# One loaded array for the input and the first block's weights, and the norm's squares two pulls later

## The chip, the cores and the metric

The kernel runs on one core of one Trainium2 chip. The metric is the device time of one execution in microseconds. Five engines work side by side, each through its own instructions in order: TensorE (PE, with its weight loads shown as PEld), VectorE (DVE), ScalarE (ACT), GpSimd (POOL) and SyncE (SP), which here issues nearly all transfers from memory.

## What is computed

One layer of a decoder trunk on 256 tokens of width 2048. All branches read the same normalised input; their gated results are summed, projected and added to the input, and a last norm closes it. Cut to what matters:

```
h = rmsnorm(x, norm_gain)
z = h @ w_in                          # split into q, k, v, gates ... of three branches
o_a = gated linear attention          # (gq, gk, gv, decay)
o_b = forgetting attention            # (fq, fk, fv, forget gate)
o_c = attention into 256 memory tokens: rmsnorm(mem) @ w_mem_kv
y = sum of sigmoid(merge) * (o_branch * silu(gate)) @ w_branch
return rmsnorm(x + y @ w_out, final_gain)
```

All data are fp32. The kernel multiplies in a reduced fp32 form and keeps the precision by splitting each operand in two: `hi` is the rounded value, `lo = raw - hi` the rest, and a product is the sum of three matmuls (hi by hi, hi by lo, lo by hi).

## The kernel before

All large products are 34 **blocks**: 512 columns of a weight matrix, 2048 rows deep, that is 16 **slices** of 128 rows (`KT`). They run in the order of the list `ORDER` (line 45); block 0 is `gq`, block 1 `gk`, blocks 2 and 3 `gv`. `wall` holds the weights as (block, 128, 16, 512). The stream works on quarters of a block (4 slices, 1 MB): `w_load` (line 144) allots a tile `raw`, of which there are 3, and SyncE loads it; `w_cast` (155) has ScalarE write `hi` of half a quarter (2 slices), `w_sub` (179) has VectorE write `lo`. There are 4 `hi` and 4 `lo` buffers. When `lo` of a quarter's second half is issued, the load three quarters ahead follows. In one engine's queue the order is that of issue in the code; SyncE sends no later load while an earlier one waits for its buffer.

`natural` (211) and `transposed` (226) are the matmul loops. `transposed` with `group=1` (block 0) does, slice by slice, four matmuls with `hi` (line 254) and four with `lo` (259), one of each per quarter of the output columns. With `group=4` (block 1) it takes four slices as a group and goes through the four output quarters; each quarter is a step of 4 matmuls with `hi` and 4 with `lo`, two of the latter from each pair of slices.

What is not a large product is written as generators in three lanes (`post`, `side`, `main`). After each slice or step the loop calls `pull()`, which takes each lane's next piece up to its `yield`; `yield 5` lets five pulls pass. So a number after `yield` sets where, between the matmuls, the next instructions are issued.

Block 0 is special: the input has to be split as well. `first_piece` (389) loads, for each pair of slices, the transposed input `xT` into a 4 KB buffer of the pool `apool` (14 of them, `a4`) and the block's weights into `raw` tiles, in two DMAs per slice or pair of slices; the first slice's weights come in two halves. ScalarE then writes the input's high part (`high_x`, line 358), scaled by the gain, and `hi` of the weights (130); VectorE the low parts (361, 131). Block 0's quarters take `raw` tiles too, so the three loads of block 1 that `w_load(6)` issues at the end of block 0's pieces wait for the tiles of quarters 1, 2 and 3.

The norm's factor per token needs the sum of squares of `x` in its natural layout (`xn`). `rms_of` (307) loads the first 128 tokens as two tiles of 128x1024, lets 5 pulls pass, squares both on ScalarE (318), loads the second 128 tokens, lets 5 pulls pass and squares these. The same routine serves the memory tokens (`memn`) about 100 us later. The results are applied behind the products (`scale_T`). Around the first squares, `post` holds the end of block 0: ScalarE copies each quarter of `gq` out (241), VectorE adds the other half (244).

The tiles tagged `m12_0` to `m12_3` (8 KB per partition each) hold the split memory tokens from `load_mem` on (374), and later the branches' outputs.

At the end, `residual` (1044) adds the input and squares with a running sum into `fs`, and `finish` (1058) makes the last norm's factor: VectorE adds the last sum to the earlier ones and scales (1066), ScalarE takes the root (1067), VectorE the reciprocal and one Newton step (1069 to 1071), and the output tiles are scaled and stored.

Of the kernel before, what the change touches and what calls it, by code (L numbers as in the profile page):

```python
# [10 lines left out]
F32 = mybir.dt.float32  # L11
# [48 lines left out]
@with_exitstack  # L60
def body(ctx, tc, xT, memT, xn, memn, wall, wsm, wup, cst, fgain, out):
    nc = tc.nc
# [81 lines left out]
    def w_load(upto):  # L144

        while done[0] <= min(upto, 4 * N_STREAM + 1):
            i, q = divmod(done[0], 4)
            raws[done[0]] = wpool.tile([P, 4, NB], F32, tag="raw", name=nm("raw"), bufs=3)
            if i == N_STREAM:
                q += 2  # L150
            if i:
                nc.sync.dma_start(raws[done[0]], wall[i, :, 4 * q:4 * q + 4, :])
            done[0] += 1

    def w_cast(upto):

        while done[1] <= min(upto, 8 * N_STREAM + 3):
# [8 lines left out]
            if q < 4:  # L166
                lo = wpool.tile([P, 2, NB], F32R, tag="lo", name=nm("lo"))
                first_piece(q, s, raws[q], hi, lo)
                done[2] += 1
                parts[n] = [hi, lo]  # L170
                if n == 7:
                    w_load(6)
            else:
                nc.scalar.copy(hi, raws[q][:, 2 * s:2 * s + 2, :])  # L174
                parts[n] = [hi]
# [131 lines left out]
    def rms_of(src, col, stage):  # L307

        ssq = spool.tile([P, NT, 2], F32, tag="ssq", name=nm("ssq"))
        for t in range(NT):  # L310
            held = []
            for c in range(2):
                raw = stage()
                nc.sync.dma_start(raw, src[:, t, c * 1024:(c + 1) * 1024])
                held.append(raw)
            yield 5
            for c in range(2):
                nc.scalar.activation(held[c], held[c], AF.Square, accum_out=ssq[:, t, c:c + 1])
                yield 1
        ms = spool.tile([P, NT], F32, tag="ms", name=nm("ms"))  # L320
# [20 lines left out]
    nc.gpsimd.memset(warm, 1.0)  # L341
    x12, xraws = [], []

# [44 lines left out]

    def first_piece(g, s, raw, hi, lo):

        if s == 0:
            xraws.append(a4([P, 4, S]))
            x12.append(new_h("x12_", g))
        step = 1 if g < 2 else 2
        for k in range(0, 2, step):
            ks = slice(2 * s + k, 2 * s + k + step)
            kts = slice(4 * g + ks.start, 4 * g + ks.stop)
            nc.sync.dma_start(xraws[g][:, ks, :], xT[:, kts, :])
            cut = (0, 256, NB) if kts.start == 0 else (0, NB)
            for a, b in zip(cut, cut[1:]):  # L400
                nc.sync.dma_start(raw[:, ks, a:b], wall[0, :, kts, a:b])
            for j in range(ks.start, ks.stop):
                kt = 4 * g + j
                high_x(x12[g], xraws[g][:, j, :], j, cs[:, C_GAIN + kt:C_GAIN + kt + 1])
                low_x(x12[g], xraws[g][:, j, :], j, cs[:, C_GAIN + kt:C_GAIN + kt + 1])
                for a, b in zip(cut, cut[1:]):
                    split_w(raw[:, j, a:b], hi[:, j - 2 * s, a:b], lo[:, j - 2 * s, a:b])
        if (g, s) == (2, 1):
            nc.sync.dma_start(wsr, wsm)
            nc.sync.dma_start(w3r, wup)  # L410
# [631 lines left out]
    fs = [cpool.tile([P, 6], F32, name=f"fs{t}") for t in range(NT)]  # L1042

    def residual(n, t, ps, sl, i):

        xt = xr[n][:, t, sl]
        nc.vector.tensor_tensor(out=xt, in0=ps, in1=xt, op=ALU.add)
        sq = a2([P, NB])
        nc.scalar.activation(sq[:, sl], xt, AF.Square, accum_out=fs[t][:, i:i + 1])
        g = fg[n // 2][:, (n % 2) * NB + sl.start:(n % 2) * NB + sl.stop]  # L1050
        nc.vector.tensor_tensor(out=xt, in0=xt, in1=g, op=ALU.mult)

    def residual_in_psum(n, t, ps, sl, i):

        sq = a2([P, NB])
        nc.scalar.activation(sq[:, sl], ps, AF.Square, accum_out=fs[t][:, i:i + 1])

    def finish(t, n_sums, last=None):

        f = spool.tile([P, 6], F32, tag="fin", name=nm("fin"))
        prev, m, neg, r, u, rr = (f[:, i:i + 1] for i in range(6))
        nc.vector.tensor_reduce(prev, fs[t][:, :n_sums - 1], AX.X, ALU.add)
        nc.vector.tensor_scalar(prev, prev, D * EPS, None, ALU.add)
        nc.vector.tensor_scalar(m, fs[t][:, n_sums - 1:n_sums], prev, 4.0 / D, ALU.add, ALU.mult)
        nc.scalar.activation(r, m, AF.Sqrt)
        nc.vector.tensor_scalar(neg, m, -1.0, None, ALU.mult)
        nc.vector.reciprocal(r, r)
# [29 lines left out]
    def late_loads():  # L1099
# [3 lines left out]
        def last_quarter(q):  # L1103

            held.append(hpool.tile([P, 4, NB], F32, tag="mx"[q] + "12_3", name=nm("lraw")))
            nc.sync.dma_start(held[q], wall[len(ORDER) - 1, :, 4 * q:4 * q + 4, :])

# [74 lines left out]
def _layout(inp):  # L1182
# [10 lines left out]
    blocks = [mats[m][:, o:o + NB] for m, o in ORDER]  # L1193
    wall = np.empty((len(blocks), P, KT, NB), np.float32)
    for i, b in enumerate(blocks):
        wall[i] = kp(b)
# [13 lines left out]
    return {  # L1210
        "xT": kp(x.T), "memT": kp(mem.T), "xn": nat(x), "memn": nat(mem), "wall": wall,
        "wsm": wsm, "wup": wup.reshape(96, 512), "cst": cst, "fgain": g["final_gain"][None, :],
# [16 lines left out]
```

## Time and profile before

| | us |
|---|---|
| median of 3 runs | 814.37 |
| lowest and highest | 813.76 and 817.84 |
| profiled execution, its own time | 814.85 |
| its span, first to last instruction | 812.6 |
| TensorE busy in it | 800.5 |
| granted TensorE clock | 0.997 |

A row of the order of time gives the start and the duration in us, the engine, the line of the kernel, the operation, output and inputs, and how many such instructions follow each other; in brackets stands how long the engine had been idle and what ended that. `SPq` is SyncE's queue: the moment at which a load is sent, not its landing. A row of the waits gives who waited for whom, the sum in us, the times and the longest.

### The profile page before, as it was taken

What the parts mean: (1) busy time and instruction counts of PE and PEld (TensorE: products, weight loads), DVE (VectorE), ACT (ScalarE), POOL (GpSimd) and SP (SyncE); (2) the same over time, 40 slices, a digit from 0 to 9 for tenths busy, and PEclk for the clock granted to TensorE, in tenths of its full rate; (3) what the DMA queues carried; (4) which work ended last, traced back from release to release, by engine and by line L of the source; (5) the groups of instructions that cost most, each with busy time, mean ns of one, the idle gap of its engine ahead of it and who ended that gap; (6) DMA issues with size and microseconds to landing.
All of it is one profiled execution on the core that took longest, in us unless ns stands there. A gap on an engine that the chain in (4) does not pass through costs nothing.

```text
span 812.6 us, 9971 instructions
## 1 busy us (share of the span) xinstructions
PE 800.5 (99%) x3888; PEld 673.5 (83%) x3888; DVE 499.0 (61%) x705; ACT 405.2 (50%) x558; POOL 22.6 (3%) x44
## 2 busy tenths in 40 slices
PE   9999999999999999999999999999999999999995
PEld 7788888888888788888888888888888888888885
DVE  6757979885656566667445744465446544575653
ACT  6758646644445465564444444444443444444631
POOL 7000000100000000000000000000000000000000
PEclk9999999999999999999999999999999999999998
DMA  8965647553443444455555455555555555548633
GB/s 279 384 238 181 233 157 253 184 197 144 156 167 145 155 160 151 161 202 193 181 196 207 161 201 208 191 179 199 196 178 196 198 177 195 207 163 308 233 125 104
DMA packets 27439, 157.31 MB, mean 194 GB/s; under 512 B 3216, under 2 KB 4640, under 8 KB 10496
## 3 DMA queue, kind: packets, MB, share of 16 engines
q1 hardware_dynamic: 27120, 156.64, 54.2%
q8 instruction: 30, 0.49, 0.2%
q14 instruction: 17, 0.14, 0.1%
q10 hardware_dynamic: 144, 0.02, 0.0%
q0 software_dynamic: 128, 0.02, 0.0%
HBM read 154.55 MB, written 2.10 MB: 193 GB/s over the span
## 4 chain that ended last, share of the span: by engine, by line
PE 91%; DVE 3%; DMA 3%; ACT 2%; issue 1%; SPq 1%; DVEq 0%; ACTq 0%
PE acc L224 19%; PE acc L226 19%; PE acc L225 19%; PE acc L254 12%; PE acc L259 6%; PE acc L1094 4%; PE acc L1093 4%; PE acc L1095 4%; DMA raw<-wall 2%; PE att L705 1%; DMA a<-xn 1%; DVE lo L187 1%; PE att L441 0%; PE att L1006 0%; PE att L782 0%
## 5 line engine op out<-in xcount | busy, mean ns | idle before, releaser
L187 DVE TENSOR_TENSOR lo<-raw,hi 128x1024 fp32r<-128x1024 f32 x256 | 312.3, 1223 | 200.0 <-ACT hi L174 199.9
L174 ACT CAST hi<-raw 128x1024 fp32r<-128x1024 f32 x256 | 266.4, 1052 | 323.0 <-PE acc L226 238.7
L224 PE MATMUL acc<-hi,x 128*128 128x512 f32 x544 | 214.8, 395 | 0.0
L225 PE MATMUL acc<-lo,x 128*128 128x512 f32 x544 | 212.0, 390 | 0.0
L226 PE MATMUL acc<-hi,x 128*128 128x512 f32 x544 | 211.9, 390 | 0.0
L226 PEld LDWEIGHTS acc<-hi,x 128*128 128x128 f32 x544 | 102.1, 188 | 21.6
L225 PEld LDWEIGHTS acc<-lo,x 128*128 128x128 f32 x544 | 102.2, 188 | 20.8 <-DVE lo L187 0.4
L224 PEld LDWEIGHTS acc<-hi,x 128*128 128x128 f32 x544 | 102.2, 188 | 20.6 <-issue 0.3
L254 PE MATMUL acc<-x,hi 128*128 128x512 f32 x384 | 108.1, 403 | 0.0
L254 PEld LDWEIGHTS acc<-x,hi 128*128 128x128 f32 x384 | 66.8, 189 | 9.9 <-issue 0.3
L259 PEld LDWEIGHTS acc<-x,lo 128*128 128x128 f32 x384 | 58.9, 188 | 10.3 <-DVE lo L187 2.1
L259 PE MATMUL acc<-x,lo 128*128 128x256 f32 x384 | 61.5, 281 | 1.7 <-DVE lo L187 1.7
L224 PE MATMUL acc<-hi,oT 128*128 128x512 f32 x128 | 49.8, 389 | 0.0
L225 PE MATMUL acc<-lo,oT 128*128 128x512 f32 x128 | 49.8, 389 | 0.0
L226 PE MATMUL acc<-hi,oT 128*128 128x512 f32 x128 | 49.8, 389 | 0.0
L1093 PE MATMUL acc<-hi,a 128*128 128x512 f32 x96 | 37.5, 391 | 0.0
L1095 PE MATMUL acc<-hi,a 128*128 128x512 f32 x96 | 37.4, 389 | 0.0
L1094 PE MATMUL acc<-lo,a 128*128 128x512 f32 x96 | 37.4, 389 | 0.0
L225 PEld LDWEIGHTS acc<-lo,oT 128*128 128x128 f32 x128 | 24.0, 188 | 5.0
L226 PEld LDWEIGHTS acc<-hi,oT 128*128 128x128 f32 x128 | 24.0, 188 | 5.0
L224 PEld LDWEIGHTS acc<-hi,oT 128*128 128x128 f32 x128 | 24.0, 188 | 5.0
L1095 PEld LDWEIGHTS acc<-hi,a 128*128 128x128 f32 x96 | 18.0, 188 | 3.8
(221 smaller groups left out, 770.1 us busy)
## 6 DMA issues: line engine op xcount, KB each, us to landing
raw<-wall SPq DMA_DIRECT2D x130, 1024.0 KB, 4.7
a<-xn SPq DMA_DIRECT2D x8, 512.0 KB, 7.5
raw<-wall SPq DMA_DIRECT2D x4, 512.0 KB, 8.0
a<-memT SPq DMA_DIRECT2D x4, 512.0 KB, 6.2
a<-memn SPq DMA_DIRECT2D x4, 512.0 KB, 7.1
lraw<-wall SPq DMA_DIRECT2D x2, 1024.0 KB, 7.5
out<-a SPq DMA_DIRECT2D x8, 256.0 KB, 3.1
raw<-wall SPq DMA_DIRECT2D x7, 256.0 KB, 4.6
```

What stands on the lines that cost most here:

```text
L174: nc.scalar.copy(hi, raws[q][:, 2 * s:2 * s + 2, :])
L187: nc.vector.tensor_tensor(out=lo, in0=raws[q][:, 2 * s:2 * s + 2, :], in1=parts[n][0].bitcast(F32), op=ALU.subtract)
L224: MM(ps[t], lhsT=h1, rhs=hi, start=(kt == first), stop=False)
L225: MM(ps[t], lhsT=h1, rhs=lo, start=False, stop=False)
L226: MM(ps[t], lhsT=h2, rhs=hi, start=False, stop=(kt == last))
L254: MM(ps[c], lhsT=hi[:, c * P:(c + 1) * P], rhs=h_of(h, kt).rearrange("p a s -> p (a s)"), start=(kt == 0), stop=False, skip_group_check=True)
L259: MM(ps[c][:, :S], lhsT=lo[:, c * P:(c + 1) * P], rhs=h_of(h, kt)[:, 0, :], start=False, stop=(kt == KT - 1), skip_group_check=True)
L705: MM(ps[:, j, :], lhsT=E[:, e * P:(e + 1) * P], rhs=Qs[c // 2][:, e % 4, :], start=True, stop=True)
L1093: MM(ps, lhsT=h1, rhs=hi, start=(kt == 0), stop=False)
L1094: MM(ps, lhsT=h1, rhs=lo, start=False, stop=False)
L1095: MM(ps, lhsT=h2, rhs=hi, start=False, stop=(kt == KT - 1))
```

## The change

The input and block 0's weights now lie side by side in one array `xw` of (128, 16, 768): per slice and partition 256 values of the input and 512 of the weights. `wall` loses block 0. `first_piece` loads them together: slice 0 in three DMAs as before (input, two halves of the weights), slices 1 to 7 in one DMA of 384 KB each, slices 8 to 15 in four of 768 KB. They land in the four places `m12_0` to `m12_3`, two slices in each, so each place is filled twice before the memory tokens come. The buffers for `xT` and block 0's use of the `raw` tiles are gone.

`rms_of` issues the second pair of loads before the first squares and holds four tiles at once: loads, 5 pulls, loads, 2 pulls, two squares, 4 pulls, two squares. The first pair of squares is thus issued two pulls later and the second pair at the pull where it stood.

`finish` gets its factor 4/D from the squares (`scale=SQ`). The square root reads the last sum directly and takes the earlier ones, with epsilon, as its bias; one VectorE operation is gone, and VectorE's negated sum stands beside the root.

```
 def w_load(upto):
         while done[0] <= min(upto, 4 * N_STREAM + 1):
             i, q = divmod(done[0], 4)
-            raws[done[0]] = wpool.tile([P, 4, NB], F32, tag="raw", name=nm("raw"), bufs=3)
...
             if i:
-                nc.sync.dma_start(raws[done[0]], wall[i, :, 4 * q:4 * q + 4, :])
+                raws[done[0]] = wpool.tile([P, 4, NB], F32, tag="raw", name=nm("raw"), bufs=3)
+                nc.sync.dma_start(raws[done[0]], wall[i - 1, :, 4 * q:4 * q + 4, :])
...
 def rms_of(src, col, stage):
-        for t in range(NT):
-            held = []
+        held = []
+        for wait in (5, 2):
+            t = len(held) // 2
             for c in range(2):
-                raw = stage()
-                nc.sync.dma_start(raw, src[:, t, c * 1024:(c + 1) * 1024])
-                held.append(raw)
-            yield 5
-            for c in range(2):
-                nc.scalar.activation(held[c], held[c], AF.Square, accum_out=ssq[:, t, c:c + 1])
-                yield 1
+                held.append(stage())
+                nc.sync.dma_start(held[-1], src[:, t, c * 1024:(c + 1) * 1024])
+            yield wait
+        for i, raw in enumerate(held):
+            nc.scalar.activation(raw, raw, AF.Square, accum_out=ssq[:, i // 2, i % 2:i % 2 + 1])
+            yield (1, 4, 1, 1)[i]
...
-    def first_piece(g, s, raw, hi, lo):
+    def first_piece(g, s, hi, lo):
...
-            xraws.append(a4([P, 4, S]))
...
+        p = 2 * g + s
+        both = hpool.tile([P, 8 * S], F32, tag=f"m12_{p % 4}", name=nm("xw"))
+        both = both[:, :6 * S].rearrange("p (k c) -> p k c", k=2)
         step = 1 if g < 2 else 2
         for k in range(0, 2, step):
-            nc.sync.dma_start(xraws[g][:, ks, :], xT[:, kts, :])
-            cut = (0, 256, NB) if kts.start == 0 else (0, NB)
+            cut = (0, S, 2 * S, 3 * S) if kts.start == 0 else (0, 3 * S)
             for a, b in zip(cut, cut[1:]):
-                nc.sync.dma_start(raw[:, ks, a:b], wall[0, :, kts, a:b])
+                nc.sync.dma_start(both[:, ks, a:b], xw[:, kts, a:b])
...
 def finish(t, n_sums, last=None):
-        nc.vector.tensor_scalar(prev, prev, D * EPS, None, ALU.add)
-        nc.vector.tensor_scalar(m, fs[t][:, n_sums - 1:n_sums], prev, 4.0 / D, ALU.add, ALU.mult)
-        nc.scalar.activation(r, m, AF.Sqrt)
-        nc.vector.tensor_scalar(neg, m, -1.0, None, ALU.mult)
+        nc.vector.tensor_scalar(prev, prev, 4.0 * EPS, None, ALU.add)
+        nc.scalar.activation(r, fs[t][:, n_sums - 1:n_sums], AF.Sqrt, bias=prev)
+        nc.vector.tensor_scalar(neg, fs[t][:, n_sums - 1:n_sums], prev, -1.0, ALU.add, ALU.mult)
```

What this moves on ScalarE at the end of block 0: before, from the first copy of `gq` (`a_109`) out of its sums (`att`) on; `hi` is a cast of block 1's weights, `a_348` and `a_350` are the first two tiles of `xn`, and `ssq` their sums of squares.

```order
L241 COPY a_109<-att_175 128x256
L174 CAST hi_425<-raw_309 128x1024
L318 ACTIVATE a_348,ssq_347<-a_348 128x1024
L241 COPY a_109<-att_177 128x256
L318 ACTIVATE a_350,ssq_347<-a_350 128x1024
L241 COPY a_109<-att_179 128x256
L241 COPY a_109<-att_181 128x256
L436 CAST w_100<-b_99 96x512
L174 CAST hi_489<-raw_311 128x1024
```

The same stretch of ScalarE after the change, where `a_337` and `a_339` are the two tiles of `xn`:

```order
L241 COPY a_109<-att_168 128x256
L174 CAST hi_414<-raw_298 128x1024
L241 COPY a_109<-att_170 128x256
L241 COPY a_109<-att_172 128x256
L318 ACTIVATE a_337,ssq_336<-a_337 128x1024
L241 COPY a_109<-att_174 128x256
L438 CAST w_100<-b_99 96x512
L318 ACTIVATE a_339,ssq_336<-a_339 128x1024
L174 CAST hi_478<-raw_300 128x1024
```

The second and third copy now stand ahead of the first square, the fourth and the cast of `w` ahead of the second. VectorE's order is the same in both kernels here.

SyncE's queue before, from the input and weights of slices 12 and 13 on; `raw_307` to `raw_311` are block 1's first three quarters, `raw_376` its last:

```order
L398 DMA a_267<-xT 128x512
L401 DMA raw_264<-wall 128x1024
L398 DMA a_267<-xT 128x512
L401 DMA raw_264<-wall 128x1024
L152 DMA raw_307<-wall 128x2048
L152 DMA raw_309<-wall 128x2048
L152 DMA raw_311<-wall 128x2048
L314 DMA a_348<-xn 128x1024
L314 DMA a_350<-xn 128x1024
L152 DMA raw_376<-wall 128x2048
L314 DMA a_468<-xn 128x1024
```

And after the change, from slices 8 and 9 on; `wsr` and `b` are the small weights:

```order
L402 DMA xw_199<-xw 128x1536
L402 DMA xw_227<-xw 128x1536
L411 DMA wsr<-wsm 128x384
L412 DMA b_99<-wup 96x512
L402 DMA xw_258<-xw 128x1536
L402 DMA xw_286<-xw 128x1536
L152 DMA raw_296<-wall 128x2048
L152 DMA raw_298<-wall 128x2048
L152 DMA raw_300<-wall 128x2048
L315 DMA a_337<-xn 128x1024
L315 DMA a_339<-xn 128x1024
L152 DMA raw_365<-wall 128x2048
```

The order of what follows block 0 is the same; the eight DMAs of its last eight slices are four. In the queue of the memory tokens' norm, the third and fourth `memn` load now stand ahead of a `raw` load that stood ahead of them.

37 lines of the change are left out of this document (19 added, 18 removed).

## The prediction

> **What bounds the kernel now.** I read the page first, then who waited for whom, then the stretches of TensorE, then the order of time around each stretch in which TensorE was not full.
>
> ```profile
> PE 800.5 (99%) x3888; PEld 673.5 (83%) x3888; DVE 499.0 (61%) x705; ACT 405.2 (50%) x558; POOL 22.6 (3%) x44
> ```
> ```profile
> PE acc L259 <- DVE lo L187: 1.7, 2, 1.4
> ```
> ```profile
> 100.00:200.00 100.00, 100.00 (x542) 1.00 0.52 182
> ```
>
> TensorE is busy for 800.5 of 812.6 us, at a granted clock of 1.00. Between 100 and 200 us (busy 100.00 of 100.00, then the clock, the DMA share, GB/s) nothing but its own matmuls counts. So whatever is to be won lies at the two ends. At the start I read the weight loads of TensorE, since the start of the first load of each step marks the rhythm:
>
> ```profile
> 4.46 1.02 PEld L254 LDWEIGHTS att<-x,hi 128*128 128x128 f32 x4 [0.27 <-issue]
> 6.73 0.77 PEld L254 LDWEIGHTS att<-x,hi 128*128 128x128 f32 x4 [0.52 <-ACT hi L130]
> 8.13 0.77 PEld L254 LDWEIGHTS att<-x,hi 128*128 128x128 f32 x4
> ...
> 28.75 0.78 PEld L254 LDWEIGHTS acc<-x,hi 128*128 128x128 f32 x4
> 30.42 0.30 PEld L259 LDWEIGHTS acc<-x,lo 128*128 128x128 f32 x2 [0.43 <-DVE lo L187]
> 30.64 0.77 PEld L254 LDWEIGHTS acc<-x,hi 128*128 128x128 f32 x4
> 34.84 0.78 PEld L254 LDWEIGHTS acc<-x,hi 128*128 128x128 f32 x4
> 37.73 0.30 PEld L259 LDWEIGHTS acc<-x,lo 128*128 128x128 f32 x2 [1.65 <-DVE lo L187]
> 37.95 0.77 PEld L254 LDWEIGHTS acc<-x,hi 128*128 128x128 f32 x4
> ```
>
> An undisturbed step (one slice of 128 input rows in block 0, one output quarter of one group in block 1) takes 8.13 - 6.73 = 1.40 us. Block 0 has 16 of them, 22.40 us, and took 28.75 - 4.46 = 24.29: **1.89 us lost**, 0.87 of it after the first slice (6.73 - 4.46 - 1.40), 1.02 spread over later ones. Block 1 loses 0.49 in its first step (30.64 - 28.75 - 1.40) and 1.71 in its fifth (37.95 - 34.84 - 1.40). In all 4.09 us. That is the most that an edit to the start can win.
>
> **Who is late.** ScalarE, VectorE and SyncE in the same stretch:
>
> ```profile
> 4.51 0.41 ACT L130 CAST hi<-raw 128x256 fp32r<-128x256 f32 x1 [0.39 <-DMA raw<-wall]
> 4.87 0.51 ACT L358 ACTIVATE x<-a,cs 128x256 fp32r<-128x256 f32 x1
> 6.06 0.62 ACT L130 CAST hi<-raw 128x512 fp32r<-128x512 f32 x1 [0.68 <-DMA raw<-wall]
> ...
> 26.92 2.00 ACT L174 CAST hi<-raw 128x1024 fp32r<-128x1024 f32 x2 [0.96 <-DVE lo L131]
> ...
> 34.31 1.06 ACT L318 ACTIVATE a<-a 128x1024 f32<-128x1024 f32 x1 [2.64 <-DMA a<-xn]
> ```
> ```profile
> 6.71 0.69 DVE L131 TENSOR_TENSOR lo<-raw,hi 128x512 fp32r<-128x512 f32 x1 [0.45 <-ACT hi L130]
> ...
> 28.00 2.36 DVE L187 TENSOR_TENSOR lo<-raw,hi 128x1024 fp32r<-128x1024 f32 x2 [1.18 <-ACT hi L174]
> ...
> 35.75 0.42 DVE L244 TENSOR_TENSOR a<-att,a 128x256 f32<-128x256 f32 x1 [2.63 <-ACT a L241]
> ...
> 36.46 1.22 DVE L187 TENSOR_TENSOR lo<-raw,hi 128x1024 fp32r<-128x1024 f32 x1
> ```
> ```profile
> 2.20 0.43 SPq L398 DMA_DIRECT2D a<-xT  x1
> 2.67 0.43 SPq L401 DMA_DIRECT2D raw<-wall  x1
> ...
> 17.12 10.07 SPq L152 DMA_DIRECT2D raw<-wall  x3
> 27.24 0.91 SPq L314 DMA_DIRECT2D a<-xn  x2
> ```
>
> In block 0 ScalarE waits for loads. At 26.92 it begins block 1's casts. The row names a VectorE result, but that result belongs to slice 15, and what the cast needs of block 0 belongs to slices 8 and 9, long done; so it waited for its own load, sent at 17.12. From that cast to the second `lo` is 30.36 - 26.92 = 3.44 us, and TensorE asked for that `lo` at 30.42 - 0.43 = 29.99, 1.24 us into block 1, and got it at 30.42: the 0.49.
>
> The 1.71 is the clearest. The third of the 1 MB loads had to wait for block 0's buffer, and the tokens `xn` stand behind it on SyncE, sent at 27.24. ScalarE therefore sits 2.64 us at the first square, 34.31. Behind the square stands the copy of `gq`'s second quarter; VectorE's sum waits for that copy until 35.75 (2.63 us idle), and `lo` of slices 6 and 7 stands behind the sum and ends at 37.68. TensorE goes on at 37.73.
>
> **The change, part by part.**
>
> *Norm's squares.* Both copies now stand ahead of the first square on ScalarE, so VectorE reaches that `lo` without any token load. By rows: the first copy can start when block 0 ends; then come one cast (1.0, half of the 2.00), the second copy (128x256, no longer than x's 0.51), and on VectorE the sum 0.42, two small operations and 1.22. That is some 4.5 us after the start of block 1, against a demand four steps and 1.24 us after it, at 6.84. The 1.71 goes, whatever the loads do, and what is late next on this path has 2 us of cover. The squares themselves cost what they did. As `xn` no longer waits for a block-0 buffer, SyncE sends it some 10 us sooner, behind three loads of 1 MB; if the first of them lands at 24.6 (below), the tokens follow 2 x 2.5 + 1.2 us later at 426 GB/s, near 31, when the copies before the square end. **-1.71.**
>
> *First slice.* Its three loads go out as before, so I leave 4.46 where it is. Slice 1 is now one load of 384 KB instead of 128 and 256, sent at 2.20, and x and weights land together; so ScalarE can no longer do x (0.51) while the weights travel. The rates by stretch (us; PE, PEld, DVE, ACT, POOL busy; clock, DMA share, GB/s):
>
> ```profile
> 2.00:8.00 6.00, 5.68 (x26) 4.80 (x26) 3.22 (x6) 3.88 (x8) 5.67 (x10) 1.00 0.89 269
> 8.00:14.00 6.00, 6.00 (x37) 5.22 (x36) 5.17 (x10) 5.22 (x11) 5.59 (x12) 1.00 1.03 354
> 14.00:20.00 6.00, 6.00 (x35) 5.05 (x34) 3.53 (x8) 3.39 (x8) 3.21 (x9) 1.00 1.02 300
> 23.00:26.00 3.00, 2.84 (x16) 2.49 (x17) 2.86 (x6) 2.96 (x7) 0.00 (x0) 1.00 1.03 426
> ```
>
> The 384 KB before it had landed at 4.51; 0.393 MB more at 269 to 354 GB/s takes 1.46 to 1.11 us, so it lands at 5.6 to 6.0. Then 0.51 + 0.62 and two handovers, 1.23 in all: TensorE starts slice 1 at 6.85 to 7.2 instead of 6.73. If the load is there when ScalarE comes free at 4.92, it is 6.15. So between 0.58 won and 0.47 lost; I take **+0.30**, nearer to the two rates than to a load that waits for nobody.
>
> *Other loads of block 0.* 27 DMAs become 16, the two small ones among them, with rows of 3 and 6 KB in memory where x had 1 and 2 KB and the weights 2 and 4. Each of the four places is filled twice, so from slice 8 on a load waits for VectorE to finish the slices that held its place; the first such wait ends with slice 1's `lo` (7.40 before, about 7.7 now). The three 1 MB loads of block 1 wait for nothing of block 0 any more. To lose nothing, block 1's first load must be there 2.26 us before block 1 starts (3.44 and a handover of 0.06, less 1.24). With 0.30 more after the first slice and no other stall, block 1 starts at 4.46 + 22.40 + 1.17 = 28.03, so it must land by 25.8. Through it travel 6.29 MB of block 0, 0.39 of small weights and 1.05 of its own: 7.73 MB from about 2.0 us on, 325 GB/s. Before, the same bytes came by 26.92, 310 GB/s. Only the first 6 us have to rise from 269 to 354 to win 0.5 MB, which is 1.6 us; from 8 to 14 us the queue reached 354 with small rows, and from 23 to 26, 426 with mostly 8 KB rows. Against it, 14 to 20 us ran at 300 with a full queue, for a reason I can't see. Landing between 23 and 26.9; I take 24.6. Then the 0.49 goes (**-0.49**), and of the 1.02 I leave 0.15 (**-0.87**).
>
> *The end.*
>
> ```profile
> 804.31 0.19 ACT L1056 ACTIVATION_READ_ACCUMULATOR b<-acc 128x1 f32 x1
> 804.78 0.20 ACT L1067 ACTIVATE fin<-fin 128x1 f32<-128x1 f32 x1 [0.28 <-DVE fin L1066]
> 805.67 0.72 ACT L1081 ACTIVATE a<-a,fin 128x512 f32<-128x512 f32 x1 [0.68 <-DVE fin L1071]
> ```
> ```profile
> 804.54 0.21 DVE L1066 TENSOR_SCALAR fin<-fs,fin 128x1 f32<-128x1 f32 x1 [5.00 <-ACT b L1056]
> 805.02 0.16 DVE L1069 RECIPROCAL fin<-fin 128x1 f32<-128x1 f32 x1
> ```
>
> The square root takes its sum straight from the accumulator, with the rest as a bias: the hop 804.54 to 804.78 leaves the chain, 0.24. A bias from memory may cost 0.10 (0.72 with a scale from memory against 0.62 for the plain 128x512 cast), and the accumulator's write must be waited for. 0.05 to 0.24; **-0.20**. The scale inside the squares is one more constant, nothing.
>
> *Memory tokens.* Their four loads now need four buffers, the last two of them other ones than before, and stand one place earlier than a weight load.
>
> ```profile
> 133.19 5.59 SPq L152 DMA_DIRECT2D raw<-wall  x2
> 138.84 0.90 SPq L314 DMA_DIRECT2D a<-memn  x2
> ```
> ```profile
> raw<-wall SPq DMA_DIRECT2D x130, 1024.0 KB, 4.7
> ```
> ```profile
> 140.29 0.65 PE att L705 x4
> ```
> ```profile
> 146.94 2.00 ACT L174 CAST hi<-raw 128x1024 fp32r<-128x1024 f32 x2 [5.54 <-PE acc L254]
> ```
>
> The last one waits for the matmuls at 140.29, so the weight load behind it (the second of the 133.19 row, sent near 138.4) goes some 3 us later. Its cast comes after the one at 146.94, which had itself idled 5.54 us for TensorE, so there are over 8.5 us less a landing of 4.7 (the page's median for 1 MB): about 4 us of cover. Nothing.
>
> **Sum:** +0.30 - 0.87 - 0.49 - 1.71 - 0.20 = -2.97. The profiled execution took 814.85 us (span 812.6), 0.48 above the median 814.37; on the median I get **811.4**.
>
> **The rivals.**
>
> *The loads come no faster.* If larger rows bring nothing, block 1's first load lands at 26.9 as now, `lo` at 30.36, and what block 0 saves is given back in block 1's first step. Only the square's 1.71 and 0.20 stay: 812.5. For it: the 300 GB/s with a full queue. Against it: the 0.89 share and 269 of the first 6 us. [...] Chance 0.18.
>
> *The places are too few: slower.* Slice 8's load goes out at 7.7 and must land by 7.03 + 7 x 1.40 - 1.23 = 15.6, in 7.9 us.
>
> ```profile
> raw<-wall SPq DMA_DIRECT2D x4, 512.0 KB, 8.0
> ```
>
> The 512 KB loads of before took 8.0 in the median, and these have 768 KB. Each further microsecond stalls TensorE by one. Past 10.9 us the stall eats the 2.97; at 12 the time is 815.5. Against it: some 2.0 MB are queued at 7.7, with its own 0.79 MB 7.9 us at 354 GB/s, and 9.3 even at 300, a loss of 1.4 that still ends below before. Chance 0.04.
>
> *All of it goes.* Slice 1 starts at 6.15, no other stall is left, the end wins 0.24: 4.09 - 0.29 + 0.24 = 4.04, so 810.3. Chance 0.16.
>
> **How the numbers follow.** My forecast has the other 0.62, with 810.6 to 812.2 of its own. The range reaches below the third rival by half a microsecond for the runs' scatter (the median's lower neighbour is 813.76, 0.6 below) and above the first by 1.0: 809.8 to 813.5, which leaves out the second rival and the tails. A change of 0.5%, 4.07 us, is about what a measurement of this kernel can tell from none; faster by more needs 810.3 or less: half of the third rival and a tenth of the forecast, 0.14, and 0.04 for scatter in the rest: 0.18. Slower by more than that needs the second rival at its worst: 0.02. The rest, 0.80, is within.
>
> **What would show it.** Right: no square ahead of the `gq` copies on ScalarE and no weight load of TensorE near 36 us waiting over a microsecond; block 1's first cast before 25.8; slice 1 near 7.0; the square root right behind the accumulator's read. Wrong: block 1's first `lo` still awaited by TensorE; the loads of slices 8 to 15 landing after their casts were due; or any wait of TensorE between 100 and 200 us.

## The result and the profile after

| | before | after |
|---|---|---|
| median of 5 runs each | 814.91 | **810.91** |
| lowest and highest | 813.76 and 817.84 | 810.85 and 811.07 |
| profiled execution, its own time | 814.85 | 810.85 |
| its span | 812.6 | 808.8 |

All in us. The ratio after to before is **0.9946**, with a 95% interval of 0.9927 to 0.9966. The profiled pair differs by 4.00 us; the rest of this section follows those 4.00.

The page of the changed kernel and its list of TensorE's waits. Each row of the waits gives the sum in us, the times and the longest:

```profile
PE 799.7 (99%) x3888; PEld 673.5 (83%) x3888; DVE 498.3 (62%) x703; ACT 404.6 (50%) x558; POOL 23.7 (3%) x44
```
```profile
PE att L355 <- DVE ones L347: 1.1, 1, 1.1
```

The one listed wait left is for the `ones` of the warm-up, ahead of block 0. The waits for block 1's `lo` are gone. TensorE's weight loads at the first steps of block 0, and at the first two and the fifth and sixth of block 1:

```profile
4.48 0.50 PEld L254 LDWEIGHTS att<-x,hi 128*128 128x128 f32 x2 [0.29 <-ACT hi L130]
...
6.99 0.76 PEld L254 LDWEIGHTS att<-x,hi 128*128 128x128 f32 x4 [0.19 <-ACT hi L130]
...
8.38 0.78 PEld L254 LDWEIGHTS att<-x,hi 128*128 128x128 f32 x4
...
28.03 0.78 PEld L254 LDWEIGHTS acc<-x,hi 128*128 128x128 f32 x4
...
29.43 0.77 PEld L254 LDWEIGHTS acc<-x,hi 128*128 128x128 f32 x4
...
33.64 0.78 PEld L254 LDWEIGHTS acc<-x,hi 128*128 128x128 f32 x4
...
35.05 0.77 PEld L254 LDWEIGHTS acc<-x,hi 128*128 128x128 f32 x4
```

The first step still takes 6.99 - 4.48 = 2.51 instead of 1.40, so 1.11 is lost there. From slice 1 to block 1 it is 28.03 - 6.99 = 21.04, which is 15 steps of 1.40: nothing lost. Block 1's first and fifth steps take 1.40 and 1.41. The sixth step begins at 35.05 instead of 37.95: **2.90 of the 4.00**.

ScalarE in the same stretch, and VectorE's `lo` that had been late:

```profile
4.88 0.40 ACT L130 CAST hi<-xw 128x256 fp32r<-128x256 f32 x1 [0.74 <-DMA xw<-xw]
...
5.85 0.51 ACT L358 ACTIVATE x<-xw,cs 128x256 fp32r<-128x256 f32 x1 [0.57 <-DMA xw<-xw]
...
24.20 2.00 ACT L174 CAST hi<-raw 128x1024 fp32r<-128x1024 f32 x2 [0.63 <-DMA raw<-wall]
...
29.21 0.64 ACT L241 COPY a<-att 128x256 f32<-128x256 f32 x2
31.17 1.06 ACT L318 ACTIVATE a<-a 128x1024 f32<-128x1024 f32 x1 [1.32 <-DMA a<-xn]
```
```profile
31.01 1.22 DVE L187 TENSOR_TENSOR lo<-raw,hi 128x1024 fp32r<-128x1024 f32 x1
```

Block 1's first cast begins at 24.20 instead of 26.92. The two copies of `gq` are done by 29.85, ahead of the square, which still waits 1.32 us for `xn` and holds up nothing. The `lo` that used to end at 37.68 ends at 32.23. SyncE sends the tokens at 16.50 instead of 27.24, since the three loads ahead of them no longer wait for block 0's tiles:

```profile
14.72 1.38 SPq L152 DMA_DIRECT2D raw<-wall  x3
16.50 1.15 SPq L315 DMA_DIRECT2D a<-xn  x2
```

The stretches (PE, PEld, DVE, ACT, POOL busy; clock, DMA share, GB/s):

```profile
2.00:8.00 6.00, 5.97 (x24) 4.83 (x24) 2.96 (x7) 3.89 (x9) 5.66 (x9) 1.00 0.95 309
8.00:14.00 6.00, 6.00 (x37) 5.27 (x36) 5.66 (x11) 4.76 (x10) 5.59 (x13) 1.00 1.03 405
14.00:20.00 6.00, 6.00 (x37) 5.25 (x36) 4.69 (x9) 4.13 (x9) 4.25 (x9) 1.00 1.03 370
23.00:26.00 3.00, 3.00 (x18) 2.64 (x17) 2.21 (x4) 2.37 (x4) 0.00 (x0) 1.00 1.02 423
```

The last column reads 309, 405, 370, 423, where it read 269, 354, 300, 426. From 8 us on the DMA share is 1.02 to 1.03 in both kernels, and more bytes pass in the stretches that hold block 0's loads; where block 1's 8 KB rows travel nothing changes.

The end of the changed kernel, with TensorE's last matmul first and the sending of the last stores at the bottom:

```profile
800.75 0.28 PE L1099 MATMUL acc<-last,a 128*128 128x256 f32 x1
...
801.35 0.19 ACT L1060 ACTIVATION_READ_ACCUMULATOR b<-acc 128x1 f32 x1
801.57 0.29 ACT L1071 ACTIVATE fin<-fs,fin 128x1 f32<-128x1 f32 x1
...
801.90 0.16 DVE L1073 RECIPROCAL fin<-fin 128x1 f32<-128x1 f32 x1
...
803.06 1.80 SPq L1088 DMA_DIRECT2D out<-a  x4
```

And two rows of before that the prediction did not show, its last matmul and its last stores:

```profile
803.71 0.28 PE L1095 MATMUL acc<-last,a 128*128 128x256 f32 x1
...
806.18 1.80 SPq L1084 DMA_DIRECT2D out<-a  x4
```

From the last matmul to the reciprocal it was 805.02 - 803.71 = 1.31 and is 1.15: 0.16 won. The hop to VectorE is gone, but the root itself takes 0.29 instead of 0.20. From the last store sent to the end of the span it was 812.6 - 807.98 = 4.62 and is 808.8 - 804.86 = 3.94: **0.68 won, at a place of which the change says nothing.** The list closes with 0.06 between the sixth step and the last matmul (the matmul moved by 2.96, the step by 2.90) and 0.20 outside the span (814.85 - 812.6 against 810.85 - 808.8): 2.90 + 0.06 + 0.16 + 0.68 + 0.20 = 4.00.

### The profile page after: what moved, and what is told of

It reads as the page before. It is cut to its first block, busy times and chain, and to the rows that moved or that the text cites. A ratio compares the mean times of both kernels' runs of the same rounds, so it can differ in the third digit from the quotient of the medians.

```text
span 808.8 us, 9948 instructions
## 1 busy us (share of the span) xinstructions
PE 799.7 (99%) x3888; PEld 673.5 (83%) x3888; DVE 498.3 (62%) x703; ACT 404.6 (50%) x558; POOL 23.7 (3%) x44
## 4 chain that ended last, share of the span: by engine, by line
PE 96%; DVE 2%; ACT 1%; issue 1%; DVEq 0%
PE acc L224 19%; PE acc L225 19%; PE acc L226 19%; PE acc L254 13%; PE acc L259 7%; PE acc L1099 4%; PE acc L1098 4%; PE acc L1097 4%; PE att L254 2%; PE att L707 1%; PE att L259 1%; DVE lo L187 1%; PE att L443 0%; PE att L1008 0%; PE att L784 0%
```

## The experiments

Each kernel was timed beside the kernel before, and the ratio is to that. Three groups ran on three chips: squares_only, finish_only, loads_only and pieces_in_two (before: 814.64 in the median), then slice1_in_two, three_places, two_arrays and longer_queue (814.52), then changed_again, old_squares, half_by_scalar and single_slices (814.81). "Lost" means what a step of TensorE took beyond 1.40 us. All differences are within about half a per cent and many intervals overlap, so the rows of the profiles carry the argument, and the times only its size.

### The change in its three parts

The theory that stands in the prediction's sum is that the parts add: the squares take away the stall of 1.71, the loads what block 0 and block 1's first step lose, and the final factor its 0.2. The rival is that the stalls have one cause, loads that come late, so that the squares and the joined loads each remove the same 1.71.

**squares_only**: the kernel before with the new order of the squares alone.

```
-        for t in range(NT):
...
-            yield 5
...
+        for wait in (5, 2):
...
+            yield wait
+        for i, raw in enumerate(held):
+            nc.scalar.activation(raw, raw, AF.Square, accum_out=ssq[:, i // 2, i % 2:i % 2 + 1])
+            yield (1, 4, 1, 1)[i]
```

> The kernel before with nothing but the new order of loads and squares in the norm. Theory 1 (each part of the change takes a stall of its own): the 1.71 us that TensorE lost at 36 us is gone, the 1.89 of block 0 and the 0.49 at block 1's first lo stay: 1.7 us under the kernel before. Theory 2 (all three stalls have one cause, loads that come late; the order of the squares only covers for it): the same 1.7 us here, as the tokens come as late as before but nothing of VectorE stands behind them. Rival: the tokens, still sent at 27.2 us, now hold up the casts behind the squares, and a stall of over 1 us comes up in group 2: less than 0.7 us gained.

Measured: 812.89 (811.72 to 814.72), ratio 0.9984 (0.9975 to 0.9993). By the ratio that is 1.3 us, by the medians 1.75. ScalarE's first square in its profile:

```profile
33.25 1.06 ACT L318 ACTIVATE a<-a 128x1024 f32<-128x1024 f32 x1 [2.19 <-DMA a<-xn]
```

The tokens still come late (33.25 against 34.31), and ScalarE sits 2.19 us for them; but the copies stand ahead of that now, and TensorE's fifth step starts at 33.74 and ends at 35.14, without a stall. So the squares alone do what the prediction said of them. This profile belongs to the second quickest of the kernel's 11 runs (811.74, 1.15 below their median), and nothing was lost in block 1's first step either, and only 0.07 between slice 1 and block 1. So the 0.49 and 1.02 in the profile of before are what one execution lost with these loads (finish_only's, next, lost 0.49 and 0.33), and not a fixed price.

**finish_only**: the kernel before with the new final factor alone.

```
-        nc.vector.tensor_scalar(m, fs[t][:, n_sums - 1:n_sums], prev, 4.0 / D, ALU.add, ALU.mult)
-        nc.scalar.activation(r, m, AF.Sqrt)
...
+        nc.scalar.activation(r, fs[t][:, n_sums - 1:n_sums], AF.Sqrt, bias=prev)
```

> The kernel before with nothing but the new factor of the last norm. Both theories: the reciprocal starts 0.15 to 0.2 us sooner after the last matmul, and the time is 0.2 us under the kernel before, too little for a verdict. Rival: the 0.7 us by which the end of the execution (last store sent to last instruction) was shorter after the change belongs to this part: 0.8 us under.

Measured: 813.80 (813.38 to 815.50), ratio 0.9994 (0.9985 to 1.0003): not to be told from no change by time. The rows show the hop that went:

```profile
804.09 0.19 ACT L1058 ACTIVATION_READ_ACCUMULATOR b<-acc 128x1 f32 x1
804.32 0.29 ACT L1069 ACTIVATE fin<-fs,fin 128x1 f32<-128x1 f32 x1
...
804.65 0.16 DVE L1071 RECIPROCAL fin<-fin 128x1 f32<-128x1 f32 x1
...
805.81 1.79 SPq L1086 DMA_DIRECT2D out<-a  x4
```

Accumulator to reciprocal takes 0.56 instead of 0.71, the same 0.15 or 0.16 as in the whole change. From the last store to the end of the span (812.3) it is still 4.70. So the 0.68 does not belong to this part. The stall in block 1's fifth step is there as well, 1.81.

**loads_only**: the changed kernel with the old squares and the old final factor, so that the loads alone are new.

```
-            nc.sync.dma_start(xraws[g][:, ks, :], xT[:, kts, :])
...
-                nc.sync.dma_start(raw[:, ks, a:b], wall[0, :, kts, a:b])
...
+                nc.sync.dma_start(both[:, ks, a:b], xw[:, kts, a:b])
```

> The change without the new order of the squares and without the new factor: only the joined loads in the memory tokens' places. Theory 1: block 0's and block 1's first stall go (2.96 with slice 1's own loss of 0.26 left, so about 1.2 to 1.4 us won), the 1.71 stays, since the copy still stands behind the first square: 1.3 us under the kernel before. Theory 2: the tokens land near 31.2 us instead of 34.3, the square ends at 32.4, the copy, the sum and the lo follow until 34.8, and TensorE asks for that lo at 34.9: nothing stalls, 2.9 us under the kernel before, all but the end's 0.2.

Measured: 811.58 (811.08 to 811.66), ratio 0.9964 (0.9951 to 0.9976), 2.9 us by the ratio. ScalarE's first square and copy, VectorE's sum and `lo` behind them, and the ends of TensorE's fourth and fifth steps, in three views of its order of time:

```profile
31.25 1.06 ACT L318 ACTIVATE a<-a 128x1024 f32<-128x1024 f32 x1 [1.82 <-DMA a<-xn]
...
32.31 0.35 ACT L241 COPY a<-att 128x256 f32<-128x256 f32 x1
```
```profile
32.70 0.42 DVE L244 TENSOR_TENSOR a<-att,a 128x256 f32<-128x256 f32 x1 [1.92 <-ACT a L241]
33.40 1.22 DVE L187 TENSOR_TENSOR lo<-raw,hi 128x1024 fp32r<-128x1024 f32 x1
```
```profile
33.76 0.77 PEld L254 LDWEIGHTS acc<-x,hi 128*128 128x128 f32 x4
35.16 0.78 PEld L254 LDWEIGHTS acc<-x,hi 128*128 128x128 f32 x4
```

The square still stands ahead of the copy, as before, and everything behind it still waits. But the tokens come at 31.25 instead of 34.31, and so `lo` ends at 34.62 instead of 37.68, about when TensorE asks for it (33.76 + 1.24 = 35.00). The fifth step takes 1.40. **The terms do not add, and the one-cause theory holds:** the 1.71 goes with either part. It is the rows that show this, and old_squares below. The times alone do not: 1.3, 0.5 and 2.9 make 4.7, the whole change brought 4.4 by its ratio and 3.7 when it was repeated (changed_again), and the intervals are wider than that difference. Nor is the 2.9 quite the 2.9 that was expected: in this profile the end took 3.93, so the 0.68 belongs to the loads, and it is in this number.

### What in the loads does it

**pieces_in_two**: the changed kernel, its array and places kept, with each piece fetched in two DMAs again (input, weights).

```
-            cut = (0, S, 2 * S, 3 * S) if kts.start == 0 else (0, 3 * S)
+            cut = (0, S, 2 * S, 3 * S) if kts.start == 0 else (0, S, 3 * S)
```

> The changed kernel, with every load of block 0 sent as two DMAs again (input, weights) out of the same joined array and into the same places: short rows of 1 and 2 KB and 27 DMAs again, but the raw tiles stay free for block 1. If the joined rows make the loads quicker (my prediction's step): the first 20 us run at about 310 to 350 GB/s, block 0 loses over 1 us again in its later slices or block 1's first lo is awaited, 0.8 to 1.5 us over the changed kernel. If what counts is that block 1's loads no longer wait for block 0's tiles: within 0.3 us of the changed kernel, slice 1 perhaps 0.2 sooner.

Measured: 812.95 (811.76 to 813.94), ratio 0.9975 (0.9962 to 0.9988). Its quickest run is above the slowest of loads_only on the same chip, though it has the other two parts as well. The profile is that of its quickest run; two stretches and a wait of TensorE:

```profile
8.00:14.00 6.00, 6.00 (x37) 5.29 (x36) 5.48 (x11) 5.52 (x12) 5.66 (x12) 1.00 1.02 359
14.00:20.00 6.00, 6.00 (x35) 5.21 (x34) 4.46 (x9) 3.89 (x9) 3.99 (x10) 1.00 1.07 348
```
```profile
PE acc L259 <- DVE lo L187: 0.2, 1, 0.2
```

From 8 to 14 us the rate is that of before again (328 to 365 GB/s in the five profiles with two DMAs for each piece, 383 to 407 in the eight with joined loads and four places), and even in this run block 1's first `lo` is awaited (0.43 lost in that step; first cast at 25.95). The places, which free block 1's loads from block 0's tiles, are the same as in the changed kernel, and by the medians the kernel is 1.7 us below before, no more than squares_only alone. So it is the joining that brings the loads' gain, and no gain of the places alone shows. Of the 2.0 us between this kernel and the changed one (812.95 and 810.91) 0.65 lie behind the last store (4.59 against 3.94 us, below). Rows of 1 to 4 KB against rows of 3 to 6 KB made 359 against 405 GB/s here.

**two_arrays**: the changed kernel's places, with `xT` and block 0's weights in separate arrays and two DMAs for each piece.

```
-                nc.sync.dma_start(both[:, ks, a:b], xw[:, kts, a:b])
+            nc.sync.dma_start(both[:, ks, :S], xT[:, kts, :])
...
+                nc.sync.dma_start(both[:, ks, a:b], w0[:, kts, a - S:b - S])
```

> The changed kernel's places and order of squares, but the input and block 0's weights in two arrays as before, two DMAs for each piece: it differs from the run with the pieces in two only in where the rows stand in memory. If side by side in memory counts by itself: over 0.5 us slower than that run's 812.9. If only the number of DMAs and the length of their rows count: within 0.5 us of it, with the same spread of about 2 us between executions.

Measured: 813.45 (812.22 to 814.77), ratio 0.9976 (0.9959 to 0.9993), as pieces_in_two. In its profiled run (814.21, one of its slower ones) the rates are below before's, and block 0 loses 2.09 behind the start of slice 1 instead of 1.02:

```profile
8.00:14.00 6.00, 5.90 (x33) 4.96 (x32) 5.26 (x10) 5.27 (x11) 5.59 (x13) 1.00 0.98 328
14.00:20.00 6.00, 4.96 (x29) 4.18 (x28) 3.13 (x7) 3.08 (x6) 3.07 (x7) 1.00 0.96 294
```

Lying side by side in memory shows no gain by itself (0.5 us by the medians, on two chips, none by the ratios); it counts because it lets one DMA do the work of two. Whether that is by the longer rows or by the smaller number of DMAs is not separated by these two, since both go together here.

**single_slices**: slices 8 to 15 as eight loads of 384 KB with rows of 3 KB, instead of four of 768 KB with 6 KB.

```
-        step = 1 if g < 2 else 2
+        step = 1
```

> The changed kernel with slices 8 to 15 sent as eight loads of 384 KB (rows of 3 KB) instead of four of 768 KB (rows of 6 KB). If rows of 3 KB are long enough, which the 405 GB/s from 8 to 14 us say: block 0 loses nothing more, within 0.2 us of the changed kernel. If the number of loads in flight or the longer rows carry the gain: slices 8 to 15 or block 1's first lo are awaited, 0.3 to 1 us over.

Measured: 811.49 (810.88 to 812.20), ratio 0.9955 (0.9940 to 0.9971), 0.25 above the unchanged copy of the changed kernel in the same group (below). In its profile nothing was lost after slice 1; the 2.09 lost ahead of it come from slice 0's second half, which stands alike in both kernels. Its end took 4.31 instead of 3.94 (below), more than the whole difference of 0.25, so rows longer than 3 KB brought nothing that shows.

**slice1_in_two**: only slice 1 in two DMAs. The prediction charged 0.30 to x and weights of slice 1 landing together.

```
-            cut = (0, S, 2 * S, 3 * S) if kts.start == 0 else (0, 3 * S)
+            cut = (0, S, 2 * S, 3 * S) if kts.start == 0 else (0, S, 3 * S) if kts.start == 1 else (0, 3 * S)
```

> The changed kernel with slice 1's 384 KB sent as two DMAs, the input first and then the weights. Theory (my step on the first slice): the 1.11 us that TensorE loses after slice 0 is longer than the 0.87 of before because x and weights land together and ScalarE's 0.51 for x comes behind the landing; sent apart, slice 1 starts near 6.5 instead of 6.99, and the time is 0.4 to 0.5 us under the changed kernel. Rival: the weights land by as much later as they are sent later, or the queue of the first six microseconds is full anyhow: less than 0.15 us.

Measured: 811.84 (811.24 to 812.41), ratio 0.9956 (0.9942 to 0.9970). TensorE's first steps:

```profile
6.64 0.75 PEld L254 LDWEIGHTS att<-x,hi 128*128 128x128 f32 x4 [0.18 <-ACT hi L130]
...
9.27 0.76 PEld L254 LDWEIGHTS att<-x,hi 128*128 128x128 f32 x4 [1.17 <-ACT hi L130]
```

Slice 1 does start sooner, 6.64 instead of 6.99, with 0.70 lost ahead of it instead of 1.11. ScalarE works on its input from 5.30 on, while the weights still travel (their cast begins at 5.97), as the step behind the 0.30 has it. But slice 2 then comes 1.23 late, and block 1 starts at 28.89 instead of 28.03. Slice 2's load is sent one DMA later, some 0.5 us; what the rest is, one profile does not tell (changed_again, with no edit, lost 0.51 one slice further on). Nothing was won: the theory that this kernel would be quicker fell.

**half_by_scalar**: the first half of slice 0's weights sent by ScalarE, ahead of its table load, so that SyncE's later loads go out 0.44 us sooner.

```
-                nc.sync.dma_start(both[:, ks, a:b], xw[:, kts, a:b])
+                first = kts.start == 0 and a == S
+                (nc.scalar if first else nc.sync).dma_start(both[:, ks, a:b], xw[:, kts, a:b])
```

> The changed kernel with the first half of slice 0's weights sent by ScalarE, ahead of its table load, instead of by SyncE, so that every later load of the start is sent 0.44 us sooner. If the first loads are held by the moment at which they are sent: slice 0's second half and slice 1 land 0.3 to 0.45 us sooner, the 1.11 us lost after slice 0 shrink to 0.7 to 0.8, and the time is 0.3 to 0.4 us under the changed kernel, the best of all. If they are held by the rate of the first six microseconds (226 GB/s from 2 to 4 us): less than 0.1 us.

Measured: 811.29 (810.82 to 812.91), ratio 0.9957 (0.9939 to 0.9975), 0.05 from the unchanged copy. In its profile 1.27 is lost after slice 0 and block 1 starts at 28.46. From 2 to 8 us 333 GB/s pass instead of 309, but ScalarE gets slice 1's input at 6.30 instead of 5.85, so the sooner sending brought slice 1 no sooner landing. The time is what was expected of loads held by the queue's rate; but since that rate rose in this profile, this is not shown.

### Places and squares beside the joined loads

**three_places**: three of the four places.

```
-        both = hpool.tile([P, 8 * S], F32, tag=f"m12_{p % 4}", name=nm("xw"))
+        both = hpool.tile([P, 8 * S], F32, tag=f"m12_{p % 3}", name=nm("xw"))
```

> The changed kernel with the loads of block 0 going through three of the four places, two slices in each. This is my rival on the places, made worse by one place. If the wait for a place can set TensorE's pace (it decides where landing takes longer than the slices held ahead): slice 6's load goes out at about 7.9 instead of 5 and lands near 13 against a demand at 12.8, slice 8's goes out near 10.3 and lands 7.0 us later, 17.3 against 16.3: 0.7 to 1.5 us lost in block 0, the time as much over the changed kernel. If the loads are held by the queue's rate alone and the places don't matter: within 0.3 us.

Measured: 812.05 (810.83 to 812.65), ratio 0.9956 (0.9939 to 0.9973). Two stretches and TensorE's wait in its profile:

```profile
8.00:14.00 6.00, 6.00 (x34) 5.25 (x35) 5.49 (x11) 4.99 (x12) 5.66 (x11) 1.00 0.94 308
14.00:20.00 6.00, 6.00 (x35) 5.20 (x35) 3.54 (x7) 2.59 (x7) 3.33 (x8) 1.00 0.97 294
```
```profile
PE att L254 <- DVE x L361: 1.9, 3, 1.2
```

With three places the queue is not full all the time (share 0.94 and 0.97 instead of 1.03), 0.62 and 0.37 are lost at slices 9 and 11, and block 1's first cast comes at 27.52. The time is some 0.8 to 1.1 above that of the changed kernel's two sets of runs, which were on other chips. The rival of too few places is a real mechanism, but it begins between three and four places, and still does not make the kernel slower than before.

**old_squares**: the changed kernel with the old order of the squares (the lines of squares_only, the other way round).

```
-        for wait in (5, 2):
...
+        for t in range(NT):
...
+            yield 5
```

> The changed kernel with the old order of loads and squares in the norm: joined loads and the new last factor stay. Theory 2 (one cause, late loads; with the loads early the order of the squares has nothing left to win): no wait of TensorE near 35 us, within 0.2 us of the changed kernel, in every execution as far as the spread shows. Theory 1 (my sum: the squares' order takes a stall of 1.71 us of its own): 1.7 us over it. Between them: the lo is ready only 0.1 us before TensorE asks for it by my reckoning, so some executions may lose a few tenths: a median 0.2 to 0.5 us over and a wider spread.

Measured: 811.45 (810.87 to 812.38), ratio 0.9956 (0.9940 to 0.9972). **changed_again** is the changed kernel once more, in the same group, as the measure for it and its neighbours:

```
(no edit)
```

> The changed kernel itself once more, on the chip of this call, as the measure for the three runs beside it. All theories: 810.9 within 0.3, and a spread between executions of a few tenths.

Measured: 811.24 (810.91 to 812.77), ratio 0.9954 (0.9939 to 0.9969). Two of its ten runs lie above 812.5, so the scatter was larger than expected. The old order costs 0.2, which is inside this scatter, where terms that add would have cost 1.7. In the profile of old_squares, the slowest of its nine runs, the late tokens hold up the square, but nothing of TensorE:

```profile
32.68 1.06 ACT L318 ACTIVATE a<-a 128x1024 f32<-128x1024 f32 x1 [1.64 <-DMA a<-xn]
```

```profile
34.83 1.22 DVE L187 TENSOR_TENSOR lo<-raw,hi 128x1024 fp32r<-128x1024 f32 x1
```
```profile
35.36 0.78 PEld L254 LDWEIGHTS acc<-x,hi 128*128 128x128 f32 x4
```

`lo` ends at 36.05, and TensorE, whose fifth step starts at 35.36, asks for it at 36.60. The margin is 0.55, and 0.38 in loads_only; in the changed kernel it is 33.64 + 1.24 - 32.23 = 2.65. Beside the joined loads the new order of the squares is a reserve of some 2 us, on which TensorE did not call in these runs.

### The 0.68 at the end

The theory: SyncE has 11 loads fewer to send in the changed kernel, and something at the end of an execution goes with the length of its program. The rival: the 0.68 is a matter of chance or of where the new tiles lie. **longer_queue** gives the changed kernel 11 tiny loads on SyncE, one behind every sixth weight load in the middle of the kernel, into a tile that nobody reads.

```
+                if done[0] >= 60 and done[0] % 6 == 0 and len(pads) < 11:
+                    pads.append(done[0])
+                    nc.sync.dma_start(pad[:, len(pads) - 1:len(pads)], cst[:, 0:1])
```

> The changed kernel with 11 loads of 4 bytes per partition added to SyncE's queue, one behind every sixth weight load from block 15 on; nobody reads them. SyncE's program is then as long as in the run with the pieces in two. Theory: the last 0.7 us of the gain (from the last store's sending to the end of the execution 3.94 us against 4.6 to 4.7) belongs to a shorter queue program, whose last piece needs one instruction fetch less (16 against 17 in the profile of the queues); with the queue longer again, 17 fetches, some 4.65 us at the end, TensorE's start and pace unchanged, 0.7 us over the changed kernel. Rival: the end is longer only by chance or through the loads at the start: 16 fetches or not, the time stays within 0.2 us of the changed kernel.

Measured: 811.88 (811.39 to 813.01), ratio 0.9961 (0.9947 to 0.9976). Its last stores, and its page's row for the queue that fetches instructions (packets, MB, share):

```profile
803.34 1.81 SPq L1093 DMA_DIRECT2D out<-a  x4
```
```profile
q14 instruction: 17, 0.14, 0.0%
```

From the last store sent to the end of the span (809.8) it is 4.65, as before. The changed kernel's own row has one packet fewer:

```profile
q14 instruction: 16, 0.13, 0.0%
```

All profiles sort by the number of block 0's loads on SyncE (with the two small weights and the 11 tiny ones). The last column is what is left of the span when the last store has landed, by the records of the traces:

| block 0's loads, with the tiny ones | kernels | last store sent to the end, us | packets of q14 | last store landed to the end, us |
|---|---|---|---|---|
| 27 | before, squares_only, finish_only, pieces_in_two, two_arrays, longer_queue | 4.59 to 4.70 | 17 | 1.61 to 1.63 |
| 20 | single_slices | 4.31 | 16 | 1.33 |
| 15 to 17 | after, loads_only, slice1_in_two, three_places, changed_again, old_squares, half_by_scalar | 3.88 to 3.99 | 16 | 0.89 to 0.95 |

So longer_queue brings the 0.68 back, and neither chance nor the place of the new tiles explains it. But the number of loads is not the cause itself. The last store lands 2.97 to 3.05 us after it was sent in every kernel; the difference lies behind that. Once the last store is sent, SyncE goes through eight waits, always in the same order, one for each of the eight semaphores (counters) on which loads and stores report their landing in turn. The list of SyncE's waits says how many of the eight still met a store under way: 2 in the kernel before, 3 in single_slices, 4 in the changed kernel, in this order:

```profile
SPq L1225 <- DMA out<-a: 3.0, 2, 2.3
```
```profile
SPq L1229 <- DMA out<-a: 2.9, 3, 1.6
```
```profile
SPq L1229 <- DMA out<-a: 2.7, 4, 0.8
```

In the changed kernel the last store's wait is the seventh of the eight, so one is left when it lands. In single_slices it is the third, and five are left; in the kernels with 27 loads it is the second, and six are left. Each that is left takes 0.06 to 0.08 us, and in every kernel with 27 loads one of them begins 0.37 to 0.39 after the one ahead of it; why that one is late stays open. Behind the eighth wait before and the changed kernel take the same, 0.84 and 0.85, so the further packet costs nothing. **What counts is the place of the last store in the turn of eight, and not how many loads there were:** 11 loads more move it by three places, and by this reading eight more would have changed nothing, which no run tried.

## Why the prediction was right, and where it was not

The time fell inside the range and near the forecast, 810.91 against 811.4 on the median. A part of that nearness is luck: the forecast was taken off 814.37, the median of three runs, and the median of five is 814.91. The change itself was 4.00 against 2.97. Of the 1.03 between them the terms of the sum make only 0.09 (2.90 + 0.16 against 2.97); the other 0.94 (0.68, 0.20 and 0.06) stood in no term. By its steps:

- **What bounds the kernel**: right. All that was won lies ahead of 36 us and behind the last matmul; the middle gave 0.06.
- **First slice, +0.30**: right in kind. Slice 1 started at 6.99 against the 7.03 that the sum used. The loss of 1.11 instead of the 1.17 worked out has a part that was not foreseen: slice 0's own second half was cast at 4.88 instead of 4.51.
- **Other loads of block 0, -0.87**: 0.15 was left to be lost, nothing was. Block 1 started at 28.03, the number worked out for no further stall (now 4.48 + 22.40 + 1.11, and 0.04 by which 15 steps are over 21.00). The condition for it, block 1's first load by 25.8, was kept with room: 24.20 against the 24.6 taken. The term was sized from the two rates of before, and 405 GB/s from 8 to 14 us went past both.
- **Block 1's first step, -0.49**: right, 1.40 after.
- **Norm's squares, -1.71**: the stall went. The step "the 1.71 goes, whatever the loads do" holds for squares_only. But taken as a term of its own it is wrong: the joined loads remove it too, and beside them the squares' order is worth 0.2 or nothing. The number came out right because the sum counted it once. Whoever had predicted the loads alone from these steps would have said 1.1 (0.87 + 0.49 - 0.30); in the profile of loads_only block 1's sixth step began 2.79 sooner (35.16 instead of 37.95).
- **The end, -0.20**: 0.16. The root with its bias from memory took 0.09 more, close to the 0.10 set for it.
- **Memory tokens, 0**: right. TensorE is busy for 100.00 of the 100 us from 100 on.
- **What the sum lacked**: 0.68 between the last store and the end of the span, and 0.20 outside it. Rows for both stood in the profile of before (stores sent by 807.98, span 812.6, own time 814.85), and the prediction took them as fixed. The first comes from the place of the last store's wait among SyncE's last eight, which the smaller number of loads happened to shift; the second is of the size of its scatter (1.8 to 2.2 in the other kernels' profiles).

Of the rivals, *the loads come no faster* fell by the rates and by loads_only. *Too few places* is real with three places and not with four. *All of it goes* gave 810.3 by other terms than those that made 810.91: slice 1 did not start at 6.15, and slice1_in_two shows that it can't be had for nothing. The chance of 0.18 for faster by more than half a per cent was low for a kernel that came out just at that border (0.9946 and 0.9954): with the 0.68 counted, the sum would have been 3.65, 0.45% of the time.

No kernel of this study beats the changed one; half_by_scalar equals it within the scatter.

## What to carry to other kernels

When several stalls stand close together, ask of each what is late *first*: if it is one queue, edits that hide a stall and edits that speed up the queue win the same microseconds, and their terms must not be added as if independent. Joining two loads of 1 to 4 KB rows into one was worth doing at the start of a kernel where the queue is full, while splitting just the one load that is needed first moved the delay to the next. The time behind the last store is part of the metric: look at what SyncE still waits for there before calling an edit's DMAs free because they are hidden in the middle, and before crediting an edit at the start with what is won at the end.

## What was not expected of the hardware

The end of an execution takes 3.9 us after the last store is sent with 15 to 17 of block 0's loads on SyncE, 4.3 with 20 and 4.6 to 4.7 with 27, though those loads were sent hundreds of microseconds earlier: they set which of SyncE's last eight waits is the last store's. And the scatter between executions is as large as what most of these edits win: the kernels with two DMAs for each piece ran from 811.76 to 813.94 and from 812.22 to 814.77, the changed one from 810.85 to 811.07 in one set of five runs and from 810.91 to 812.77 in another of ten. That it depends on the form of the loads is not shown. In the profiles it is slice 0 and the steps behind it that differ (1.1 to 2.1 us lost ahead of slice 1 in the seven whose loads for slices 0 and 1 are the same).
